# Where the second branch's gate sums meet the tokens' factor: at the PSUM eviction, or after their return from DRAM

## Chip, cores and metric

The kernel runs on one core of one Trainium2 chip. The metric is the device time of one execution in microseconds, taken as the median of the runs; lower is better.

## What is computed

The reference is one layer of a decoder trunk: 512 tokens, 1024 channels, fp32. Cut to what matters here:

```python
h = rms_norm(x, norm_mix)
proj = h @ w_in                      # split into rq, rk, rv, rg, cq, ckv, krope, gr, gm
a_ret = (rms_norm(retention(rq, rk, rv)) * silu(rg)) @ w_br
a_mla = attention(cq, ckv, krope) @ w_bm
mixed = sigmoid(gr) * a_ret + sigmoid(gm) * a_mla
x = x + mixed @ w_o                  # then an MLP, then a gated input embedding
```

`rms_norm` multiplies each token's row by one number, the reciprocal root of its mean square, and each channel by a gain. The kernel uses that a token's factor can be taken out of a product: it multiplies `w_in` by x with the gains only, and applies the factor to the result. In the kernel the tensors lie turned, channels on the 128 partitions and the 512 tokens along the free axis, so the tokens' factor is a full 128x512 tile, `rbc`, whose rows are all alike. The change concerns `gm`, the gate of the attention branch: 1024 channels, that is eight tiles of 128x512.

## The kernel before

Every matrix product is made of three TensorE products: each operand is split into a high and a low part (`split` for activations, lines 302 to 314; `load_chunk` for weights, lines 247 to 269), and `mm3` (line 292) multiplies low by high, high by low and high by high, recorded as line 169. For each chunk of weights ScalarE writes the high part (`wh_...`, line 262) and VectorE the low part (`wl_...`, line 266). So TensorE waits for ScalarE and then VectorE ahead of each chunk, unless they are early. Three weight chunks can be in their split form at a time (`NW`), six in the raw form.

The work is a list of steps in one order (`step`, `fill`, lines 1181 to 1414). First come the latent projections, then the attention heads, two at a time. Between the parts of the attention the list puts "fillers" (line 1181): the half products of the gates `gm` and `gr`, which depend on nothing but x and their weights, so that TensorE has work while VectorE and ScalarE do the softmax. `gate_m` (line 679) adds up one gate tile in a PSUM bank in two such halves. After the second half `gate_out` (line 686) empties the bank into an SBUF tile `zm`, and `aside` (line 352) writes that to DRAM with a DMA issued by GpSimd. Tile 0 is the exception: its products come before the factor `rbc` exists, so its `gate_out` is a step of its own, after `x_factor` (line 460), which makes `rbc` with a ScalarE copy.

When all heads are done, `branch_m` (line 694) runs eight times: it loads one gate tile back from DRAM over SyncE's queue into a tile `gb`, takes the sigmoid on ScalarE, multiplies it by the branch's product `bm` in PSUM on VectorE and puts the result aside again (`am`). Between these steps `norm_x` (line 708) normalises x with `rbc` for the retention part that follows. `rbc` is also used by `gate_r` (line 903) for the other gate.

Three things set the order. TensorE's matmuls, the sines and the sigmoid of `branch_m` are wrapped in `keep_in_program_order` and stay in the order of the list. All other instructions are placed by the tile framework's planner when the program is built: each engine gets one fixed queue, in which an instruction that the planner thought ready may stand ahead of one that is written earlier. And an SBUF tile of the pool `dyn` (45 tiles of 128x512, handed out by `T`) or a PSUM bank (8, handed out by `B`) is free again only when its last reader is done, a DMA among them.

Other names that the prediction uses: `v00h`, `v00l` and the like are the split attention values (line 542); `o`, `qt`, `sa`, `sb` belong to the rotation of the queries (`rotary_out`, lines 550 to 570), which runs once for each group of four heads; `tra` and `trs`, `trc` are the angles and their sine and cosine for the retention part (`trig`, lines 466 to 480, and `sincos`, line 486); `hr` and `nsc` are a pair of heads' factors (`pair_stats`, line 591), `kf` is a head's factor for the keys (line 613); `sc` the scores, `p` and `mx` the scaled scores and their maximum (line 644), `pt` the turned probabilities; `sqk` a square of the keys (line 527).

Of the kernel before, what the change touches and what calls it, by code (L numbers as in the profile page):

```python
# [33 lines left out]
AF = mybir.ActivationFunctionType  # L34
ALU = mybir.AluOpType
# [113 lines left out]
def trunk_layer(ctx: ExitStack, tc: tile.TileContext, xT, pT, pos, gains, const, decay, wstream, outT):  # L149
# [15 lines left out]
    TT, STT, TS = nc.vector.tensor_tensor, nc.vector.scalar_tensor_tensor, nc.vector.tensor_scalar  # L165
    ACT = nc.scalar.activation
# [4 lines left out]
    def T(name, dtype=F32):  # L171
        return dyn.tile([P, S], dtype, tag="t", name=name)
# [4 lines left out]
    def B(name):  # L177
        return psum.tile([P, S], F32, tag="ps", name=name)
# [113 lines left out]
    def mm3(ps, stat, mov, first, last, **k):  # L292

        (sh, sl), (mh, ml) = stat, mov
        MM(ps, sl, mh, start=first, stop=False, **k)
        MM(ps, sh, ml, start=False, stop=False, **k)
        MM(ps, sh, mh, start=False, stop=last, **k)

    def cut(pair, a, n=P):
        return pair[0][:, a:a + n], pair[1][:, a:a + n]  # L300
# [15 lines left out]
    def proj(ps, acts, w, base=0, stride=P, k0=0, k1=None):  # L316

        n = len(acts)
        for k in range(k0, n if k1 is None else k1):
            mm3(ps, cut(w, base + (k - k0) * stride), acts[k], k == 0, k == n - 1)  # L320
        return ps
# [28 lines left out]
    V = {}  # L350

    def aside(name, t):

        d = spill.tile([P, S], F32, tag=name, name=name + "d")
        nc.gpsimd.dma_start(d, t)
        return d
# [320 lines left out]
    gate_ps = {}  # L677

    def gate_m(w, n, half):
        if half == 0:  # L680
            gate_ps[n] = B(f"gm{n}")
        proj(gate_ps[n], xg, w, k0=4 * half, k1=4 * half + 4)
        if half == 1 and n:
            gate_out(n)

    def gate_out(n):
        t = T(f"zm{n}")
        TT(t, gate_ps[n], V["rbc"], op=ALU.mult)
        zm[n] = aside(f"zm{n}", t)

    def mo_split(h):
# [2 lines left out]
    def branch_m(w, n):  # L694
        t = T(f"gb{n}")
        nc.sync.dma_start(t, zm[n])
        ps = proj(B(f"bm{n}"), mo, w)
        tc.keep_in_program_order(ACT(t, t, AF.Sigmoid))
        TT(t, t, ps, op=ALU.mult)
        zm[n] = aside(f"am{n}", t)  # L700
# [503 lines left out]
    step(("v", 0), value_pair, 0)  # L1204
    step(None, x_factor)
    step(None, gate_out, 0)
    step(("qr", 0), query_rotary, 0)
    step(None, mask_parts)
# [66 lines left out]
    for n in range(8):  # L1275
        step(("bm", n), branch_m, n)
        if n < 6:
            step(None, norm_x, 2 + n)
        if n == 3:
            step(None, x_operand, 7)  # L1280
# [177 lines left out]
```

## Time and profile before

| what | value |
|---|---|
| median of 3 runs | 1101.72 us (1101.19 to 1101.97) |
| the profiled execution, its own time | 1101.0 us |
| its span, first to last instruction | 1099.2 us |
| mean granted TensorE clock | 0.999 |
| VectorE busy | 757.9 us, 69% of the span |
| ScalarE busy | 565.8 us, 51% |
| GpSimd busy | 111.1 us, 10% |

The profile is one execution, with every instruction's start and duration in microseconds from the span's start. Engines are PE (TensorE; PEld is its weight load), DVE (VectorE), ACT (ScalarE), POOL (GpSimd) and SP (SyncE, which issues DMAs; SPq is its queue). A row names the line of the kernel, the operation, out<-in, and shapes. In rows of the timeline the first number is the start, the second the duration, and a bracket at the end gives how long the engine had been idle and what ended the wait. Rows of groups have a count (x8), the busy time and the mean duration in ns. Matmuls are pipelined, so that a duration is longer than the step from one to the next.

### The profile page before, as it was taken

Reading aid. Unit: us, or ns where it says so; the run is one execution under the profiler, and the core shown is the slowest. Engines: PE = TensorE matmul, PEld = TensorE weight load, DVE = VectorE, ACT = ScalarE, POOL = GpSimd, SP = SyncE. Lnnn points to the kernel's source line nnn. Section 1 sums busy time; section 2 is a strip of 40 time slices with the busy share of each in tenths; the row PEclk is TensorE's granted clock in tenths of the full one; section 3 lists DMA queues with packets and bytes.
Section 4 is the critical chain, followed back from the end, with each engine's and each line's share of the span. In section 5 each row is a group of like instructions: output and inputs, shape, how many; then the busy total and the mean of one; then the engine's idle time right before and its main releaser. Section 6 shows DMA issues by size and latency. Waiting matters only on the chain. (4 is left out here: it accounts for less than half of the span.)

```text
span 1099.2 us, 14887 instructions
## 1 busy us (share of the span) xinstructions
PE 1085.2 (99%) x5569; PEld 923.3 (84%) x5569; DVE 757.9 (69%) x1176; ACT 565.8 (51%) x817; POOL 111.1 (10%) x145
## 2 busy tenths in 40 slices
PE   9999999999999999999999999999999999999998
PEld 7778888888888888888888888887899899898887
DVE  7697677566774655655465467649869769769784
ACT  7647656444466545344554644426645545546541
POOL 0000000000112001122100100011111111201000
PEclk9999999999999999999999999999999999999999
DMA  7232231356778744498864934694998999979511
GB/s 261 71 120 87 72 107 50 133 199 212 206 190 241 193 157 159 121 196 213 204 205 118 286 126 148 199 305 117 229 267 222 229 272 220 238 217 279 154 47 58
DMA packets 64616, 195.91 MB, mean 178 GB/s; under 512 B 7904, under 2 KB 9312, under 8 KB 64160
## 3 DMA queue, kind: packets, MB, share of 16 engines
q1 hardware_dynamic: 46464, 134.90, 35.7%
q0 software_dynamic: 17936, 60.04, 27.3%
q8 instruction: 44, 0.72, 0.3%
q14 instruction: 28, 0.23, 0.1%
q10 hardware_dynamic: 144, 0.03, 0.0%
HBM read 175.80 MB, written 17.04 MB: 175 GB/s over the span
## 5 line engine op out<-in xcount | busy, mean ns | idle before, releaser
L169 PE MATMUL dn<-wl_dn,ch 128*128 128x512 f32 x224 | 87.7, 391 | 1.5 <-DVE wl_dn L266 1.5
L169 PE MATMUL dn<-wh_dn,cl 128*128 128x512 f32 x224 | 87.7, 391 | 1.4 <-DVE cl L308 0.9
L169 PE MATMUL dn<-wh_dn,ch 128*128 128x512 f32 x224 | 87.2, 389 | 0.0
L262 ACT ACTIVATE wh_up<-wr_up 128x1024 fp32r<-128x1024 f32 x32 | 33.9, 1058 | 44.1 <-PE us L169 13.4
L266 DVE TENSOR_TENSOR wl_up<-wr_up,wh_up 128x1024 fp32r<-128x1024 f32 x32 | 39.1, 1221 | 24.4 <-ACT wh_up L262 24.0
L262 ACT ACTIVATE wh_dn<-wr_dn 128x1024 fp32r<-128x1024 f32 x32 | 33.9, 1059 | 34.1 <-PE us L169 16.5
L169 PEld LDWEIGHTS dn<-wh_dn,cl 128*128 128x128 f32 x224 | 42.1, 188 | 10.5 <-DVE cl L308 1.3
L169 PEld LDWEIGHTS dn<-wl_dn,ch 128*128 128x128 f32 x224 | 42.1, 188 | 10.3 <-DVE wl_dn L266 2.3
L169 PEld LDWEIGHTS dn<-wh_dn,ch 128*128 128x128 f32 x224 | 42.1, 188 | 8.8
L266 DVE TENSOR_TENSOR wl_dn<-wr_dn,wh_dn 128x1024 fp32r<-128x1024 f32 x32 | 39.0, 1220 | 10.7 <-ACT wh_dn L262 10.6
L262 ACT ACTIVATE wh_rv<-wr_rv 128x1024 fp32r<-128x1024 f32 x28 | 29.7, 1059 | 30.6 <-issue 9.9
L262 ACT ACTIVATE wh_rg<-wr_rg 128x1024 fp32r<-128x1024 f32 x28 | 29.6, 1059 | 30.4 <-PE rg L169 12.1
L266 DVE TENSOR_TENSOR wl_rg<-wr_rg,wh_rg 128x1024 fp32r<-128x1024 f32 x20 | 24.5, 1226 | 23.5 <-ACT wh_rg L262 23.4
L224 POOL DMA_DIRECT2D dr_dn<-wstream x24 | 21.9, 957 | 173.2 <-DVE rx L331 95.9
L266 DVE TENSOR_TENSOR wl_dn<-dr_dn,wh_dn 128x1024 fp32r<-128x1024 f32 x24 | 29.3, 1220 | 13.9 <-ACT wh_dn L262 13.9
L266 DVE TENSOR_TENSOR wl_rv<-wr_rv,wh_rv 128x1024 fp32r<-128x1024 f32 x20 | 24.4, 1223 | 16.2 <-ACT wh_rv L262 16.2
L266 DVE TENSOR_TENSOR wl_br<-wr_br,wh_br 128x1024 fp32r<-128x1024 f32 x16 | 19.5, 1221 | 19.7 <-ACT wh_br L262 19.7
L1105 DVE TENSOR_TENSOR d<-d,dn 128x1024 f32<-128x1024 f32 x24 | 29.2, 1217 | 5.4 <-PE dn L169 5.4
L262 ACT ACTIVATE wh_up<-dr_up 128x1024 fp32r<-128x1024 f32 x18 | 19.1, 1062 | 25.9 <-PE dn L169 14.1
L262 ACT ACTIVATE wh_dn<-dr_dn 128x1024 fp32r<-128x1024 f32 x24 | 25.3, 1053 | 13.1 <-PE dn L169 6.5
L262 ACT ACTIVATE wh_br<-wr_br 128x1024 fp32r<-128x1024 f32 x16 | 16.9, 1058 | 21.0 <-issue 12.8
L873 ACT ACTIVATE rt<-br 128x512 f32<-128x512 f32 x24 | 13.9, 594 | 25.8 <-PE br L169 25.8
(1889 smaller groups left out, 3690.2 us busy)
## 6 DMA issues: line engine op xcount, KB each, us to landing
wr_up<-wstream SPq DMA_DIRECT2D x32, 512.0 KB, 5.6
wr_dn<-wstream SPq DMA_DIRECT2D x32, 512.0 KB, 6.9
dr_dn<-wstream POOLq DMA_DIRECT2D x24, 512.0 KB, 9.5
wr_rv<-wstream SPq DMA_DIRECT2D x20, 512.0 KB, 4.1
wr_rg<-wstream SPq DMA_DIRECT2D x20, 512.0 KB, 5.0
dr_up<-wstream POOLq DMA_DIRECT2D x18, 512.0 KB, 9.0
wr_rv<-wstream POOLq DMA_DIRECT2D x16, 512.0 KB, 6.5
wr_rg<-wstream POOLq DMA_DIRECT2D x16, 512.0 KB, 6.9
```

Of the source, the lines that this page charges most:

```text
L169: return tc.keep_in_program_order(nc.tensor.matmul(*a, **k))
L224: nc.gpsimd.dma_start(raw, chunk(("w", blk, kb, fb, c)), accum_op=ALU.add)
L262: i = ACT(hi, raw, AF.Copy, scale=sign)
L266: TT(lo, raw, hi.bitcast(F32), op=ALU.subtract)
L873: ACT(t, ps, AF.Copy)
L1105: TT(to, to, dps[p], op=ALU.add if sign > 0 else ALU.subtract)
```

## The change

`gate_out` no longer multiplies by `rbc` on VectorE as it empties the bank; ScalarE copies the sums as they are, and they go to DRAM so. `branch_m` multiplies the tile by `rbc` on VectorE after it is back in SBUF, ahead of the sigmoid. Nothing else is edited; the step that empties tile 0 stays after `x_factor`, though its copy no longer reads `rbc`.

```diff
     def gate_out(n):
         t = T(f"zm{n}")
-        TT(t, gate_ps[n], V["rbc"], op=ALU.mult)
+        ACT(t, gate_ps[n], AF.Copy)
         zm[n] = aside(f"zm{n}", t)
...
     def branch_m(w, n):
         t = T(f"gb{n}")
         nc.sync.dma_start(t, zm[n])
+        TT(t, t, V["rbc"], op=ALU.mult)
         ps = proj(B(f"bm{n}"), mo, w)
         tc.keep_in_program_order(ACT(t, t, AF.Sigmoid))
         TT(t, t, ps, op=ALU.mult)
```

## The prediction

> **What bounds the kernel now.** I read the page first: engine shares and the granted clock.
>
> ```profile
> PE 1085.2 (99%) x5569; PEld 923.3 (84%) x5569; DVE 757.9 (69%) x1176; ACT 565.8 (51%) x817; POOL 111.1 (10%) x145
> ...
> PEclk9999999999999999999999999999999999999999
> ```
>
> TensorE is busy 99% at full clock; no instruction of its is touched. The change can gain only TensorE's idle time, 14.0 us of the span of 1099.2. Next I asked for TensorE's waits in the stretch where the gate tiles are made (40 to 149 us), and for busy time by stage: us of the stage, then PE, PEld, DVE, ACT.
>
> ```profile
> PE gm L169 <- DVE wl_gm L266: 1.6, 1, 1.6
> PE sc L169 <- ACT sqk L527: 0.8, 1, 0.8
> PE pt0a L169 <- DVE p L653: 0.6, 1, 0.6
> PE gm L169 <- DVE mx L644: 0.6, 1, 0.6
> ```
>
> ```profile
> 90.00:103.00 13.00, 11.55 (x63) 9.69 (x62) 10.65 (x30) 12.31 (x26) 0.00 (x0) 1.00 0.21 62
> ...
> 285.00:738.00 453.00, 453.00 (x2067) 377.87 (x2066) 271.05 (x396) 221.63 (x324) 52.15 (x66) 1.00 0.68 190
> 738.00:775.00 37.00, 34.34 (x167) 28.02 (x166) 36.01 (x42) 24.43 (x30) 3.48 (x4) 1.00 0.59 153
> ```
>
> Four waits, 3.6 us together, lie where VectorE loses the eight multiplications. From 285 to 738 us TensorE is never idle, and where the multiplications come back (232 to 283 us) its waits list nothing either: what is saved or lost ahead shifts the rest unchanged, and added VectorE work costs nothing unless it outlasts its cover.
>
> **What moves, and its price.** The instruction that leaves and those that resemble what comes:
>
> ```profile
> L688 DVE TENSOR_TENSOR zm<-gm,rbc x8: 681/692/692, 61.7 to 176.4; 128x512 f32<-128x512 f32 x8
> ```
>
> ```profile
> 61.09 0.60 ACT L463 ACTIVATE rbc<-prx 128x512 f32<-128x512 f32 x1
> 61.57 0.49 ACT L310 ACTIVATE v00h<-pv,f 128x256 fp32r<-128x256 f32 x1
> ...
> 62.28 0.62 ACT L553 ACTIVATE sa<-pqa 128x512 f32<-128x512 f32 x1
> ```
>
> ```profile
> 61.27 0.48 DVE L313 SCALAR_TENSOR_TENSOR v01l<-pv,f,v01h 128x256 fp32r<-128x256 f32 x1
> 61.72 0.69 DVE L688 TENSOR_TENSOR zm<-gm,rbc 128x512 f32<-128x512 f32 x1
> 62.33 0.48 DVE L313 SCALAR_TENSOR_TENSOR v00l<-pv,f,v00h 128x256 fp32r<-128x256 f32 x1
> ...
> 63.11 0.74 DVE L556 SCALAR_TENSOR_TENSOR o<-pqa,gn,tmc 128x512 f32<-128x512 f32 x1
> ...
> 65.74 0.68 DVE L560 TENSOR_TENSOR o<-o,qt 128x512 f32<-128x512 f32 x1
> ...
> 68.15 0.68 DVE L266 TENSOR_TENSOR wl_gm<-wr_gm,wh_gm 128x512 fp32r<-128x512 f32 x1
> ```
>
> ```profile
> 68.98 0.47 PE L169 MATMUL gm<-xg0h,wl_gm 128*128 128x512 f32 x1 [1.56 <-DVE wl_gm L266]
> ```
>
> A multiplication holds VectorE 0.61 us (61.72 to the next start at 62.33); eight free 4.9 us ahead of 177 us. Eight return in branch_m, at 0.6 to 0.7 each by the SBUF row of 65.74. ScalarE gains eight copies out of PSUM: `rbc` is such a copy, and the next instruction starts 0.48 us after it, so 3.8 us. Engine totals do not set the end; the four waits do.
>
> *First wait (68.98).* VectorE works without a break from 61.27, and the weights' low part is last in that queue, at 68.15. With zm0 gone it could come 0.61 sooner, but v00l then waits for ScalarE's v00h (61.57 + 0.49 = 62.06 against its start at 62.33), and `o` for `sa`, which reads the same product and ends at 62.90 against 63.11. I take 0.2, between 0 and 0.6. The copy itself needs no `rbc`, and tile 0's last product starts at 45.19, so the planner can place it 15 us earlier; if it stays among these rows it takes the 0.2 back.
>
> ```profile
> 45.19 0.39 PE L169 MATMUL gm<-xg7h,wh_gm 128*128 128x512 f32 x1
> ...
> 112.26 0.39 PE L169 MATMUL gm<-xg7h,wh_gm 128*128 128x512 f32 x1
> ```
>
> *Second and third waits.* One chain ends both.
>
> ```profile
> 82.21 0.17 DVE L605 TENSOR_SCALAR nsc<-hr 128x8 f32<-128x8 f32 x1
> 82.68 0.69 DVE L688 TENSOR_TENSOR zm<-gm,rbc 128x512 f32<-128x512 f32 x1 [0.30 <-PE gm L169]
> 83.29 0.48 DVE L468 TENSOR_SCALAR tra<-posf,cst 128x512 f32<-128x512 f32 x1
> ...
> 88.10 0.43 DVE L479 TENSOR_SCALAR tra<-tra 128x512 f32<-128x512 f32 x1
> ```
>
> ```profile
> 88.57 0.63 ACT L487 ACTIVATE trs<-tra 128x512 f32<-128x512 f32 x1 [5.21 <-DVE tra L479]
> ...
> 89.62 0.58 ACT L613 ACTIVATE kf<-pbk 128x512 f32<-128x512 f32 x1
> ...
> 100.28 0.61 ACT L527 ACTIVATE sqk<-pk 128x512 f32<-128x512 f32 x1
> ```
>
> ```profile
> 97.39 0.66 PE L169 MATMUL pt0a<-cst,p 128*128 128x128 f32 x4 [0.65 <-DVE p L653]
> ...
> 100.94 0.45 PE L169 MATMUL sc<-k1h,q1l 128*128 128x384 f32 x1 [0.81 <-ACT sqk L527]
> ```
>
> zm3 stands ahead of the angle chain (82.68), having waited 0.30 for its bank. ScalarE waits 5.21 us for that chain and then works almost without pause (12.31 of 13 us from 90 to 103), with `kf`, the softmax and `sqk` behind it; TensorE waits for these at 97.39 and 100.94. Without zm3 the angles can start when nsc is done, at 82.3 instead of 83.29: the whole chain 1.0 us earlier. TensorE can use that: ahead by 0.2 from the first wait, it has 0.65 + 0.81 = 1.46 idle here, so 1.66 is the most without a better first wait. I take 1.0 in all at 101 us (this includes the first 0.2), between 0 (a tile slot for `tra` comes free no sooner) and 2.0. No gate copy falls among ScalarE's 90 to 103 us: zm3's is due at 82.5, inside the 5.21 idle, and zm4's last product starts only at 112.26 (the second row above).
>
> *Fourth wait.* Here the copy may hurt.
>
> ```profile
> 137.82 0.69 DVE L688 TENSOR_TENSOR zm<-gm,rbc 128x512 f32<-128x512 f32 x1 [0.30 <-PE gm L169]
> ...
> 141.40 0.75 DVE L556 SCALAR_TENSOR_TENSOR o<-pqa,gn,tmc 128x512 f32<-128x512 f32 x1 [2.23 <-DMA zm5d<-zm]
> ```
>
> ```profile
> 137.82 0.64 ACT L262 ACTIVATE wh_gm<-wr_gm 128x512 fp32r<-128x512 f32 x1 [1.20 <-PE gm L169]
> ...
> 140.97 0.59 ACT L554 ACTIVATE sb<-pqb 128x512 f32<-128x512 f32 x1
> ```
>
> ```profile
> 138.80 0.54 POOL L355 DMA_DIRECT2D zm5d<-zm  x1 [24.59 <-DVE zm L688]
> ```
>
> ```profile
> 148.09 0.47 PE L169 MATMUL gm<-xg0h,wl_gm 128*128 128x512 f32 x1 [0.65 <-DVE mx L644]
> ```
>
> `o` takes over zm5's tile and waits 2.23 us until the DMA has emptied it; nine VectorE steps later the maximum `mx` is what TensorE waits for. On ScalarE the copy becomes ready at the same moment as wh_gm, which is written earlier and goes first: 0.54 later, less 0.09 because a copy is 0.60 and not 0.69 long, gives 0.45 more wait. Between a gain of 0.65 (`o` gets another tile) and a loss of 3.75 (the copy goes behind `sb`, ending at 141.56: a rival below). I take a loss of 0.45.
>
> *branch_m.* The added multiplication stands between the load and the sigmoid, and VectorE's queue waits with it for the landing.
>
> ```profile
> 259.69 1.22 DVE L266 TENSOR_TENSOR wl_bm<-wr_bm,wh_bm 128x1024 fp32r<-128x1024 f32 x1 [2.34 <-ACT wh_bm L262]
> ```
>
> ```profile
> L169 PE MATMUL bm<-mos0h,wl_bm x8: 389/389/396, 231.1 to 269.2; 128*128 128x512 f32 x8
> ```
>
> ```profile
> DMA to landing us min/median/max: 2.7/4.2/5.9
> ```
>
> The last branch's weights, split at 260.9, are first used at 269.2, and the reload landed within 5.9 (rows of bm and of gb): 8.3 us of cover, against 0.6 plus at most the slowest landing, 5.9, which sum to 6.5. Cost nothing; were the cover gone, a tile would cost 0.6. Behind the multiplication queue x's splits and the next low parts, ahead of the same cover. `rbc` keeps its tile some 6 us longer (last read by the last branch_m, not norm_x); no wait for a tile is listed there, so nothing, at most one such load.
>
> The Trainium skill, "VectorE: DVE Perf Modes", Rules for kernel authors, speaks against the edit: work on a matmul's output should be done from PSUM directly, or after a copy only if many operations follow. One follows here, so by it the sum would be 0 saved on VectorE and 3.8 us more on ScalarE. "Perfetto Trace Analysis", Optimizing Scalar/DVE Operations, speaks for it: move work to ScalarE where VectorE is saturated. The trace bears out the second from 61.27 to 68.83 and neither elsewhere, since TensorE covers it.
>
> *Sum.* Profiled execution 1101.0 (span 1099.2 and 1.8 around it), less 1.0, plus 0.45: 1100.45. The runs' median lies 0.72 above that execution: 1101.2.
>
> **Rivals.** *All four waits go:* with VectorE lighter the planner puts the angles or `kf` sooner, and `o` takes another tile. For it: TensorE's scores are ready long before `kf`. Against: three separate bits of luck. 3.6 us less: 1098.1.
>
> *Slower, the late copy of zm5:* the planner puts it behind `sb`, at 141.56 instead of 137.82. `o`, which needs its tile, follows 3.75 us later, and TensorE at 148.09 too: 1101.0 - 1.0 + 3.75 + 0.72 = 1104.5. It decides once the copy is over 3.2 us late. For it: `o` already waits. Against: from the end of wh_gm at 138.46 to `sb` at 140.97 ScalarE has only one other instruction, `sa`.
>
> *Given back:* `tra` still waits for its tile, the first wait stays, zm5 costs 0.45: 0 to 0.5 more, 1101.7 to 1102.2.
>
> *Another order far on:* from 738 to 775 us VectorE is full (36.01 of 37) and TensorE idle 2.66. If the planner's list differs there, that may vanish, on top of the sum 1098.5, or double, on top of no gain 1101.0 + 2.66 + 0.72 = 1104.4.
>
> *A table load for each copy* would cost far more, but the trace has `rbc`, a copy, between two sines with no load listed, so nothing is left for it.
>
> **Numbers.** The forecast has 0.50, given back 0.15, all waits gone 0.14, late copy 0.10, another order 0.11 (half each way). This kernel's measurement tells about 0.2% from no change, 2.2 us: faster is below 1099.5, slower above 1103.9. Faster 0.14 + 0.05 = 0.19, slower 0.10 + 0.06 = 0.16, within 0.65. The range runs from 1098.5 to 1104.0; it leaves out the late copy, the other order's slower half and the far end of the first rival.
>
> **What would show it.** Right: in TensorE's waits the one of 1.6 shrinks a little, those of 0.6 and 0.8 by about 0.8 together, `trs` starts near 87.6; `o` still waits for zm5's DMA, a little longer; no wait from 149 to 738 us; zm0 is copied before 60 us. Wrong: a new wait in 230 to 285 us, ScalarE copies ahead of `kf` or `sqk` that delay them, `o` no longer waiting for a DMA, or the 738 to 775 stretch with other idle time than 2.66.

## The result, and the profile after

| | before | changed |
|---|---|---|
| median of 11 runs each, on one chip | 1101.55 us (1100.96 to 1102.85) | 1104.31 us (1103.12 to 1107.3) |
| ratio, 95% interval | | 1.0027 (1.0018 to 1.0036) |
| the profiled execution's span | 1099.2 us | 1103.8 us |

The changed kernel is slower by 2.8 us. The forecast was 1101.2, within a range of 1098.5 to 1104.0; it was wrong, by a loss that it had priced at nothing.

The page of the changed kernel, busy times and granted clock:

```profile
PE 1087.5 (99%) x5569; PEld 924.3 (84%) x5569; DVE 758.5 (69%) x1176; ACT 570.7 (52%) x825; POOL 110.8 (10%) x145
...
PEclk9999999999999999999999999999999999999999
```

Nothing shows here: VectorE has as much to do as before (eight multiplications out, eight in), ScalarE 4.9 us more. TensorE's waits from 40 to 149 us, where the multiplications left:

```profile
PE gm L169 <- DVE wl_gm L266: 1.9, 1, 1.9
PE sc L169 <- ACT sqk L527: 0.8, 1, 0.8
PE gm L169 <- DVE mx L644: 0.4, 1, 0.4
PE pt0a L169 <- DVE p L653: 0.2, 1, 0.2
```

In order of time, the second of the four (`pt0a`) and the fourth (`mx`) shrank, and the first grew. And from 149 to 738 us, where there was no wait at all before:

```profile
PE rq L169 <- ACT xn7h L307: 2.4, 1, 2.4
...
PE rq L169 <- DVE xn7l L308: 0.2, 1, 0.2
```

`rq` is the first product of the retention part; its operand is the normalized x, eight tiles, and it waits for the last of them. The timeline of VectorE, then ScalarE, then TensorE there, each row with the start, the duration and in brackets the idle time and what ended it:

```profile
279.95 0.69 DVE L697 TENSOR_TENSOR gb<-gb,rbc 128x512 f32<-128x512 f32 x1 [2.08 <-DMA gb<-zm5d]
281.13 0.75 DVE L713 SCALAR_TENSOR_TENSOR xr<-xr,gn,rbc 128x512 f32<-128x512 f32 x1 [0.48 <-DMA xr<-xT]
...
282.57 0.69 DVE L308 TENSOR_TENSOR xn7l<-xr,xn7h 128x512 fp32r<-128x512 f32 x1
```

```profile
280.68 0.63 ACT L699 ACTIVATE gb<-gb 128x512 f32<-128x512 f32 x1 [4.07 <-DVE gb L697]
281.91 0.63 ACT L307 ACTIVATE xn7h<-xr 128x512 fp32r<-128x512 f32 x1 [0.60 <-DVE xr L713]
```

```profile
282.60 0.50 PE L169 MATMUL rq<-xn7h,wl_rq 128*128 128x512 f32 x1 [2.37 <-ACT xn7h L307]
283.32 0.50 PE L169 MATMUL rq<-xn7l,wh_rq 128*128 128x512 f32 x1 [0.22 <-DVE xn7l L308]
```

Two things could be meant by these rows. VectorE stands 2.08 us at the new multiplication until gate tile 5 has landed, and ScalarE 4.07 us behind it at the sigmoid: the added instruction holds both queues. But right after it x's own last tile, xr7, is waited for too (0.48): it also came late. SyncE's queue says why. The kernel before, then the changed one:

```profile
266.82 0.37 SPq L696 DMA_DIRECT2D gb<-zm5d  x1
267.29 0.38 SPq L711 DMA_DIRECT2D xr<-xT  x1
```

```profile
272.89 0.41 SPq L696 DMA_DIRECT2D gb<-zm5d  x1
273.41 0.55 SPq L712 DMA_DIRECT2D xr<-xT  x1
```

Loads go out in a rhythm of one weight chunk in some 5.4 us, a gate tile and an x tile behind most of them. In the changed kernel's queue the pair stands one chunk further back. And there it also takes longer. Issues with KB and us to landing, from the stretch after the pair's issue, of the kernel before and of the changed one:

```profile
gb<-zm5d SPq DMA_DIRECT2D x1, 256.0 KB, 3.7
xr<-xT SPq DMA_DIRECT2D x1, 256.0 KB, 4.2
```

```profile
wr_rv<-wstream POOLq DMA_DIRECT2D x1, 512.0 KB, 6.6
gb<-zm5d SPq DMA_DIRECT2D x1, 256.0 KB, 7.0
xr<-xT SPq DMA_DIRECT2D x1, 256.0 KB, 7.7
am4d<-gb POOLq DMA_DIRECT2D x1, 256.0 KB, 6.2
```

Issued 6.1 us later and landed 3.5 us slower, xr7 is there at 281.1 instead of 271.5. In the changed kernel the DMA engines' share (the last column but one) reaches 1.00 while it is on its way:

```profile
274.00:278.00 4.00, 4.00 (x19) 3.33 (x18) 3.72 (x7) 1.42 (x2) 0.56 (x1) 1.00 0.96 265
278.00:282.00 4.00, 2.23 (x10) 1.50 (x8) 1.56 (x3) 0.72 (x2) 0.88 (x1) 1.00 1.00 383
```

The kernel before has as full a stretch there (1.02 from 274 to 278 us), but its xr7 had landed at 271.5, ahead of it.

The Trainium skill, "DMA: Bandwidth & Descriptors", Issuing engines are not separate DMA queues, says that DMAs of SyncE, ScalarE and GpSimd end on the same 16 engines and interleave; the rows agree, as GpSimd's two transfers here are slow as well (6.6 and 6.2; their like behind the earlier load took 5.3 and 3.9).

A measure that all kernels share is the stretch from the first matmul of `rq` (xn0h) to the first of `rk` (xn0h): 274.66 to 285.54 before, 10.88 us; 275.30 to 289.39 after, 14.09 us. That is 3.21 more: the 2.6 of waits, and a slow restart (the two matmuls above lie 0.72 apart, 0.22 of it idle, where the undisturbed step is 0.23).

The rest of the changed kernel's profiled time is in two other places. At 68.97 the longer first wait is followed by a lower clock, the column after POOL's:

```profile
68.00:72.00 4.00, 3.03 (x10) 2.45 (x11) 3.94 (x7) 0.60 (x2) 0.56 (x1) 0.79 0.55 163
72.00:76.00 4.00, 4.00 (x22) 2.76 (x22) 1.70 (x6) 0.71 (x2) 0.00 (x0) 0.78 0.41 102
```

The first experiment has the same wait without a lower clock, so the wait does not bring it in every execution; whether it brings it more often is taken up at the end. And between 742 and 764 us 0.6 us are lost, whose cause the same experiment shows.

### The profile page after: what moved, and what is told of

Read it like the earlier page. It is cut to its first block, busy times and chain, and to the rows that moved or that the text cites. A ratio compares the mean times of both kernels' runs of the same rounds, so it can differ in the third digit from the quotient of the medians.

```text
span 1103.8 us, 14884 instructions
## 1 busy us (share of the span) xinstructions
PE 1087.5 (99%) x5569; PEld 924.3 (84%) x5569; DVE 758.5 (69%) x1176; ACT 570.7 (52%) x825; POOL 110.8 (10%) x145
```

## The experiments

Two theories stood. **L**: the loads of x's tiles go out a weight chunk later, and that alone makes xr7 late. **M**: the multiplication holds VectorE and the sigmoid until the gate tile has landed, and xn7 queues behind. The first expectations call the two together A, the multiplication in `branch_m` as the cause. Rivals to both: the copies on ScalarE (**B**), and VectorE's added work as such (**W**). Twelve kernels ran on three chips, four at a time beside the kernel before (medians there 1102.11, 1101.56 and 1101.82 us), with eleven runs each, and five or six for four of them (multiplication behind the sigmoid, first copy early, x early first attempt, both early).

**One half of the change alone: the copies.** From the changed kernel:

```diff
         nc.sync.dma_start(t, zm[n])
-        TT(t, t, V["rbc"], op=ALU.mult)
         ps = proj(B(f"bm{n}"), mo, w)
```

> The copies on ScalarE as in the changed kernel, the multiplication in branch_m left out (so the factor is missing ahead of the sigmoid). Theory A, the 2.6 us idle ahead of rq come from the multiplication in branch_m alone: no wait at rq, first wait (at 68 us) still 1.9 instead of 1.6, angle chain still earlier: 1101 to 1102 where the granted clock keeps at 0.999, and some 1.7 us more in the runs in which it falls behind the longer first wait, as it did in about half of the runs of the changed kernel; median 1101.0 to 1103. Rival B, the copies on ScalarE shift the whole order of the loads: the 2.6 at rq stay, 1103.5 to 1104.5.

Measured: 1102.06 us, ratio 1.0001 (0.9992 to 1.0010), no wait from 149 to 738 us, the stretch 10.88. B falls. This kernel has no lowered clock at 68 us, so what the copies do is clean here. First wait, angle chain (VectorE, ScalarE), and the waits behind it:

```profile
68.98 0.47 PE L169 MATMUL gm<-xg0h,wl_gm 128*128 128x512 f32 x1 [1.89 <-DVE wl_gm L266]
96.91 0.66 PE L169 MATMUL pt0a<-cst,p 128*128 128x128 f32 x4 [0.21 <-DVE p L653]
100.45 0.44 PE L169 MATMUL sc<-k1h,q1l 128*128 128x384 f32 x1 [0.81 <-ACT sqk L527]
...
147.38 0.47 PE L169 MATMUL gm<-xg0h,wl_gm 128*128 128x512 f32 x1 [0.43 <-DVE mx L644]
```

```profile
81.47 0.83 DVE L266 TENSOR_TENSOR wl_kq<-wr_kq,wh_kq 128x640 fp32r<-128x640 f32 x1 [0.28 <-issue]
82.21 0.48 DVE L468 TENSOR_SCALAR tra<-posf,cst 128x512 f32<-128x512 f32 x1
...
140.61 0.75 DVE L556 SCALAR_TENSOR_TENSOR o<-pqa,gn,tmc 128x512 f32<-128x512 f32 x1 [1.44 <-ACT sa L553]
```

```profile
61.96 0.63 ACT L688 ACTIVATE zm<-gm 128x512 f32<-128x512 f32 x1
62.43 0.64 ACT L553 ACTIVATE sa<-pqa 128x512 f32<-128x512 f32 x1
...
87.50 0.63 ACT L487 ACTIVATE trs<-tra 128x512 f32<-128x512 f32 x1 [3.74 <-DVE tra L479]
...
137.32 0.60 ACT L688 ACTIVATE zm<-gm 128x512 f32<-128x512 f32 x1 [1.19 <-PE gm L169]
137.82 0.62 ACT L262 ACTIVATE wh_gm<-wr_gm 128x512 fp32r<-128x512 f32 x1
```

Against the kernel before, TensorE is 0.49 us ahead at the third wait (100.94), 0.71 at the fourth (148.09), and 0.96 at the first matmul of `rq` (274.66 to 273.70); it stays 0.97 ahead until 742 us. Then it loses most of it again, by 764 us. VectorE in the kernel before and in this one, then TensorE in both:

```profile
738.99 0.75 DVE L994 SCALAR_TENSOR_TENSOR x2n<-x2n,gn,bcx 128x512 f32<-128x512 f32 x1 [2.32 <-DMA x2n<-x2d]
```

```profile
738.87 0.75 DVE L994 SCALAR_TENSOR_TENSOR x2n<-x2n,gn,bcx 128x512 f32<-128x512 f32 x1 [2.28 <-DMA x2n<-x2d]
```

```profile
763.88 0.50 PE L169 MATMUL dn<-wl_dn,ch 128*128 128x512 f32 x1 [1.50 <-DVE wl_dn L266]
```

```profile
763.76 0.50 PE L169 MATMUL dn<-wl_dn,ch 128*128 128x512 f32 x1 [1.51 <-DVE wl_dn L266]
```

The same matmul starts 0.12 earlier, not 0.97. VectorE's rows say why. `x2n`, an operand of the MLP, is loaded back from DRAM; VectorE stands idle until it has landed, and then works without a pause up to the low part that this matmul waits for. The two loads of x2n were issued 0.96 us earlier (719.39 against 720.35), but took 16.5 us to land (median) against 15.7, so VectorE's row, too, starts only 0.12 earlier. In the profiles of all fourteen kernels this row and this matmul are shifted against the kernel before by the same amount, to 0.02 us: the changed kernel by 4.49 and 4.50, the control below by 1.06 and 1.07. So this stage starts when the load lands, and what TensorE gained ahead is lost there unless the load lands sooner as well. Why the landing moves from kernel to kernel, the runs don't show.

The two rows of TensorE also show that the clock isn't decided by the length of a wait alone: after 1.50 and 1.51 us of the same wait, the next 4 us had the full clock in the kernel before and 0.57 here.

```profile
764.00:768.00 4.00, 4.00 (x17) 3.10 (x18) 4.00 (x5) 4.00 (x5) 2.62 (x3) 1.00 0.43 71
```

```profile
764.00:768.00 4.00, 4.00 (x12) 3.09 (x12) 4.00 (x5) 4.00 (x5) 2.61 (x3) 0.57 0.51 60
```

**The other half alone: the multiplication.** From the changed kernel:

```diff
-        ACT(t, gate_ps[n], AF.Copy)
+        TT(t, gate_ps[n], V["rbc"], op=ALU.mult)
         zm[n] = aside(f"zm{n}", t)
```

> The gate sums multiplied on VectorE as before, and the changed kernel's multiplication in branch_m as well (so the factor is applied twice). Theory A: wait at rq 2.4 + 0.2 as in the changed kernel, first wait 1.6 as before, granted clock 0.999 in every run: 1104.0 to 1104.5. Rival B: no wait at rq, 1101.5.

Measured: 1103.93 us, ratio 1.0017 (1.0008 to 1.0026). xr7 goes out at 273.39 and takes 6.1 us; the wait at `rq` is 0.7 + 0.2 in the profiled execution, the stretch 12.41. So this half carries the loss, some 1.9 of 3.0 us by the ratios; the wait is smaller than expected because the load landed 1.6 us sooner than in the changed kernel.

**The multiplication behind the sigmoid.** From the last kernel:

```diff
-        TT(t, t, V["rbc"], op=ALU.mult)
         ps = proj(B(f"bm{n}"), mo, w)
         tc.keep_in_program_order(ACT(t, t, AF.Sigmoid))
         TT(t, t, ps, op=ALU.mult)
+        TT(t, t, V["rbc"], op=ALU.mult)
```

> As the run with the multiplication alone, but it stands behind the sigmoid, on the product with the branch's matmul (so the factor is applied twice, the second time in the wrong place): VectorE has the same eight extra multiplications in the same stretch, and rbc is held as long, but nothing stands between the load and the sigmoid. Theory A1, what costs is that VectorE and the sigmoid wait for the load's landing and the loads are put behind a weight chunk: no wait at rq over 0.3, 1101.5. Rival A2, the extra 5 us of VectorE's work and the longer hold of rbc's tile are the cost: wait at rq 0.6 to 2.6, 1102 to 1104.

Measured: 1105.07 us, ratio 1.0031 (1.0019 to 1.0042), wait 1.1 + 0.4, stretch 12.96. A1 falls as it was put. But the run does not prove A2 either: here too xr7 went out late, at 272.83, with no multiplication ahead of the sigmoid. Any extra VectorE step in the branch, it seems, moves the loads; so the loads had to be moved by themselves.

**Loads late, no multiplication.** From the kernel before:

```diff
     for n in range(8):
         step(("bm", n), branch_m, n)
-        if n < 6:
-            step(None, norm_x, 2 + n)
-        if n == 3:
+        if 0 < n < 7:
+            step(None, norm_x, 1 + n)
+        if n == 4:
             step(None, x_operand, 7)
```

> The kernel before, without any multiplication in branch_m, but with each norm_x from the fourth tile on one branch later, so that the load of xr7 is issued one weight chunk (some 5.5 us) later, near 273, as in the changed kernel, while the loads of the gate tiles keep their places. Theory L, what TensorE waits for at rq is the late load of xr7 and nothing else: wait at rq 0.7 to 2.6 without a single multiplication, 1102.3 to 1104.5. Rival M, it is the multiplication that holds VectorE and the sigmoid until gb5 has landed: no wait at rq over 0.3, 1101.5 to 1102.

Measured: 1104.03 us, ratio 1.0027 (1.0018 to 1.0035), the changed kernel's own ratio, without one of its edits. The loads of this kernel, and its waits from 149 to 738 us:

```profile
266.29 0.37 SPq L696 DMA_DIRECT2D gb<-zm5d  x1
...
272.51 0.49 SPq L711 DMA_DIRECT2D xr<-xT  x1
```

```profile
PE rq L169 <- ACT xn7h L307: 1.9, 1, 1.9
PE rq L169 <- DVE xn7l L308: 0.2, 1, 0.2
```

This is what L forecast, and M isn't needed for the loss. The edit delays the normalization of x together with its load; the runs below with the loads in steps of their own move the load alone.

**Gate tile early, x late.** In the changed kernel the load of `gb` becomes a step of its own, one branch ahead:

```diff
...
+    step(None, gate_in, 0)
     for n in range(8):
+        if n < 7:
+            step(None, gate_in, n + 1)
         step(("bm", n), branch_m, n)
```

> The changed kernel with the load of each gate tile one branch earlier, so that the multiplication finds gb5 landed (issued near 267), while xr7 is still loaded near 273. Theory L: wait at rq still 0.7 to 2.6, near the changed kernel, 1103 to 1104.3. Rival M: the wait at rq goes, below 0.3, and the time falls to 1101.2 to 1102.

Measured: 1103.95 us, ratio 1.0018 (1.0009 to 1.0027), wait 1.3 + 0.4. With gb5 landed long before, VectorE waits for x itself:

```profile
278.80 0.75 DVE L716 SCALAR_TENSOR_TENSOR xr<-xr,gn,rbc 128x512 f32<-128x512 f32 x1 [2.21 <-DMA xr<-xT]
279.47 0.68 DVE L700 TENSOR_TENSOR gb<-gb,rbc 128x512 f32<-128x512 f32 x1
```

M falls: the multiplication now stands behind the late tile, and the wait is still there.

**x early, first attempt.** In the changed kernel:

```diff
+    step(None, norm_x, 2)
     for n in range(8):
         step(("bm", n), branch_m, n)
-        if n < 6:
-            step(None, norm_x, 2 + n)
+        if n < 5:
+            step(None, norm_x, 3 + n)
```

> The changed kernel with norm_x one branch earlier: xr7 is loaded near 267 as in the kernel before and normalized ahead of gb5's multiplication, while gb5 is still loaded near 273 and the eight multiplications stand where they did. Theory L: no wait at rq over 0.3, 1101 to 1102. Theory M as well, as far as gb5's multiplication no longer stands ahead of xr7. Rival W, VectorE's added work of 5 us is the cost: wait at rq 0.5 to 2.6, 1102 to 1104.

Measured: 1106.67 us, ratio 1.0043 (1.0030 to 1.0055). The edit did not do what it was made for: xr7 went out at 272.50, and the wait was 1.0 + 0.2. It also made waits of 2.4 us in all for `rv`'s weights, which no other kernel has. As a test of the theories it says only that late loads go with the wait.

**x early, second attempt.** In the changed kernel the loads of x and of the gate tiles become steps of their own; `branch_m` and `norm_x` take the loaded tile, and keep the multiplication:

```diff
...
+    for k in range(2):
+        step(None, load_x, k)
     step(None, norm_x, 0)
     step(None, norm_x, 1)
     step(None, mo_split, MH - 1)
+    for n in range(2):
+        step(None, gate_in, n)
     for n in range(8):
         step(("bm", n), branch_m, n)
+        if n + 2 < 8:
+            step(None, gate_in, n + 2)
+        if n + 2 < 8:
+            step(None, load_x, n + 2)
         if n < 6:
             step(None, norm_x, 2 + n)
```

> The changed kernel with nothing but the loads of branch_m and norm_x in steps of their own, x two and the gate tiles two branches ahead: all eight multiplications stay, xr7 is put behind the same weight chunk as in the kernel before (issued near 267), gb5 earlier than there. Theory L, the late load of xr7 is the whole cost: no wait at rq over 0.3, first wait still 1.9, 1100.5 to 1102.3, within 0.2% of the kernel before. Rival M or W, the multiplication or VectorE's added work costs by itself: wait at rq 0.5 or more, 1102.5 to 1104.

Measured: 1101.82 us, ratio 1.0003 (0.9994 to 1.0012). No wait from 149 to 738 us, the stretch 10.88. x's load, and VectorE there:

```profile
266.95 0.33 SPq L716 DMA_DIRECT2D xr<-xT  x1
```

```profile
270.00 0.69 DVE L700 TENSOR_TENSOR gb<-gb,rbc 128x512 f32<-128x512 f32 x1 [0.47 <-DMA gb<-zm7d]
...
271.75 0.74 DVE L721 SCALAR_TENSOR_TENSOR xr<-xr,gn,rbc 128x512 f32<-128x512 f32 x1
```

All eight multiplications are there, VectorE even waits 0.47 for a landing, and the loss is gone. L holds; M and W fall.

> As the last run, with the gate tiles loaded one branch ahead instead of two; xr7 then goes out one weight chunk ahead of its place in the kernel before (near 262). Theory L: as the last run, no wait at rq, 1100.5 to 1102.3; the place of gb's load makes no difference. Rival M: 1102.5 to 1104.

The same, with the gate tiles one branch ahead:

```diff
-    for n in range(2):
+    for n in range(1):
         step(None, gate_in, n)
...
-        if n + 2 < 8:
-            step(None, gate_in, n + 2)
+        if n + 1 < 8:
+            step(None, gate_in, n + 1)
```

Measured: 1101.86 us, ratio 1.0004 (0.9995 to 1.0013), xr7 at 262.57, stretch 10.88. Where the gate tile's load stands makes no difference. This kernel and that of "Gate tile early, x late" both load the gate tiles one branch ahead and keep all eight multiplications; they differ in the place of x's loads alone, and their ratios are 1.0004 and 1.0018.

> The kernel before with the same early loads, without the change: the control for the three above. If the early loads are worth nothing where no load is late: 1101.5, within 0.1% of the kernel before, and the run with the loads back minus this one is what the change itself is worth, between -1 and +0.5 us. If they help or hurt elsewhere, this one shows by how much.

The control, the same edit as in the run that brought the loads back, in the kernel before, whose `branch_m` has no multiplication. Measured: 1102.24 us, ratio 1.0002 (0.9993 to 1.0010), stretch 10.88. So the early loads are worth nothing that can be measured where none was late, and neither is the change without its late loads.

**Tile 0's copy.** Three kernels moved it. Early, as soon as its product is done:

```diff
-        if half == 1 and n:
+        if half == 1:
             gate_out(n)
...
     step(None, x_factor)
-    step(None, gate_out, 0)
```

> The changed kernel, but tile 0 is copied as soon as its product is done, some 15 us earlier, and no longer ahead of sa. Theory C, the copy among those rows lengthens the first wait by 0.3 and the longer wait lets the granted clock fall in half of the runs: first wait 1.6 or less, granted clock 0.999 in every run, 1103 to 1103.7 with the 2.6 at rq unchanged. Rival D, the clock falls for another reason (heavier draw, or chance): the runs still split into two groups, some 1.7 us apart.

Measured: 1105.66 us, ratio 1.0041 (1.0027 to 1.0054). The first wait did shrink to 1.3, but 2.2 at `rq` stayed, and two waits appeared far on:

```profile
PE up L169 <- DVE wl_up L266: 2.3, 1, 2.3
...
PE up L169 <- DVE xr L935: 0.8, 1, 0.8
```

The longer one comes from the reload of x2n: it was issued at 723.10, took 18.9 us, and VectorE stood idle 5.95 us for it (2.93 in the kernel before). The runs do not split into two groups (clock 0.998 in four of five, 0.996 in one), but the 0.999 that C forecast came in none of the five, and in the profiled one the clock fell behind the wait of 2.3: neither C nor D is shown. Late, behind `sa` and `sb`, with the loads as in the run that brought them back:

```diff
-    step(None, gate_out, 0)
...
     step(None, rotary_out, 0)
+    step(None, gate_out, 0)
```

> The loads as two runs above, and tile 0's copy put behind sa and sb. If the copy ahead of sa is what made the first wait longer: first wait 1.6 or less, no wait at rq, 0.3 us less than two runs above, 1100.2 to 1102; if the rows of VectorE decide: 1.9 unchanged.

Measured: 1101.54 us, ratio 1.0002 (0.9993 to 1.0011). The wait for the weights became one of 1.4 for the copy itself, since TensorE needs the bank, and 0.3 appeared behind it: 1.7 for 1.9.

> The last run's edit together with tile 0's early copy: the version that should be best by theory L. First wait 1.3, no wait at rq, 1100.5 to 1101.5, if the new wait of 2.3 + 0.8 us at up (740 to 750 us), which the early copy alone had, came from the planner's order and not from the early copy; 1103 to 1104 if it stays.

The early copy's edit together with that of the failed first attempt. Measured: 1108.98 us, ratio 1.0061 (1.0049 to 1.0074), the slowest of all. xr7 went out at 272.34 again, a wait of 2.7 with a clock of 0.50 to 0.67 behind it, and `up` waited 2.5.

All kernels side by side, from their SyncE, DMA and TensorE rows; the issue of xr7 is counted from the first matmul of `rq`:

| kernel | multiplication in branch_m | xr7 issued, us | us to landing | stretch rq to rk, us | ratio to before |
|---|---|---|---|---|---|
| before | no | -7.4 | 4.2 | 10.88 | 1 |
| changed | yes | -1.9 | 7.7 | 14.09 | 1.0027 |
| copies alone | no | -7.4 | 4.1 | 10.88 | 1.0001 |
| multiplication alone | yes | -1.9 | 6.1 | 12.41 | 1.0017 |
| behind the sigmoid | after it | -1.9 | 6.5 | 12.96 | 1.0031 |
| first copy early | yes | -1.9 | 7.4 | 13.70 | 1.0041 |
| loads late | no | -1.6 | 6.6 | 13.63 | 1.0027 |
| gate load early | yes | -1.9 | 6.6 | 13.15 | 1.0018 |
| x early, failed | yes | -1.6 | 6.0 | 12.64 | 1.0043 |
| both early | yes | -1.8 | 7.9 | 17.09 | 1.0061 |
| loads back | yes | -7.1 | 4.1 | 10.88 | 1.0003 |
| loads ahead | yes | -11.4 | 4.2 | 10.88 | 1.0004 |
| loads back, copy late | yes | -7.1 | 3.9 | 10.88 | 1.0002 |
| before, loads ahead | no | -11.7 | 4.2 | 10.88 | 1.0002 |

The stretch follows the third column and not the second. Among the late ones it also follows the landing. Third and fourth column together give the time at which xr7 is there, counted from the first matmul of `rq`; its own first product is due 4.76 us after that matmul, and the tile must be normalized and split before. It is there at 4.2 us in the multiplication alone, then 4.4, 4.6, 4.7, 5.0, 5.5, 5.8 and 6.1 (both early), and the stretch grows in the same order, 12.41, 12.64, 12.96, 13.15, 13.63, 13.70, 14.09 and 17.09. What the runs don't settle is how an added VectorE step leads the planner to put the loads behind one more weight chunk. No version beats the kernel before.

## Why the prediction was wrong

**The step that failed** is "Cost nothing" for `branch_m`. Its cover, 8.3 us, was computed for the branch's own weights, `wl_bm`, and those were indeed early. The late operand was another one, x's last tile, which `norm_x` loads over the same queue of SyncE. "Behind the multiplication queue x's splits" was written, but x's own load was not followed: that it went out at 267.29, 7.4 us ahead of `rq`, and that its place in SyncE's queue depended on what the planner made of the branch. The price of that is 3.2 us in the profiled execution. The list of what would prove the prediction wrong named it first, a new wait in 230 to 285 us; none of the rivals did. "Another order" was looked for at 738 us, where VectorE is full, and came in SyncE's queue.

**The eviction's side was about right in its sum**, -0.55 at the fourth wait against -0.71 measured, but from terms that were each off, so that the nearness of the sum is in part luck. The first wait: the copy stayed among those rows and, as the prediction said for that case, took the gain back; `wl_gm` starts at 68.15 as before, TensorE arrives 0.32 earlier and waits that much longer. The angles: `trs` came at 87.50, forecast near 87.6, but half of the 1.0 reached TensorE (0.49), because the wait for `sqk` kept its 0.81. The place that zm3 left in VectorE's queue was taken by a split, `wl_kq`, at 81.47, which had stood ahead of `nsc` before. The fourth wait: 0.45 more was forecast, 0.22 less came. The copy of zm5 went ahead of `wh_gm`, not behind it, so `o` waits for `sa` and no longer for the DMA.

**"What is saved or lost ahead shifts the rest unchanged"** held from 285 to 742 us (0.97 throughout, copies alone) and failed behind it: at 764 us 0.12 was left. The prediction quoted 36.01 of 37 us on VectorE as a stage that is full, but did not ask what that work starts on. It starts on the reload of x2n, which TensorE's coming 0.97 sooner moved by 0.12. That is the same omission as in `branch_m`: a load of the next stage that was not followed.

So the 2.8 us are 3.2 for the late load, less 0.97, plus some 0.6 behind the reload of x2n (3.85 behind at `rk`, 2.24 without 1.61 of low clock, and 0.65 more by 763.88). The 1.61 is the distance of the changed kernel's `pt0a` (98.52) from that of the copies alone (96.91).

Of the two rules that were weighed, the Trainium skill's "Perfetto Trace Analysis", Optimizing Scalar/DVE Operations (move work to ScalarE where VectorE is saturated) was right for 61 to 148 us, by 0.71. The Trainium skill's "VectorE: DVE Perf Modes", Rules for kernel authors, spoke against the edit, and the edit lost, but not for its reason: with the loads back, the extra step costs nothing that can be measured (1.0003, 0.9994 to 1.0012).

## What to carry to other kernels

When an instruction is added to a stage, ask for every operand of the next stage's first products when its load goes out and when it lands, not only for the operand that the added instruction touches; a load that is ready 7 us early is covered by its place in the queue, and the place can move. If loads and their use are one step, give the loads a step of their own. And a gain ahead of a stage that starts when a load lands is a gain at the end only as far as that load lands sooner too.

## What the runs showed of the hardware

A 256 KB load took 3.9 to 4.2 us when issued 7 us or more ahead of `rq`, and 6.0 to 7.9 when issued 1.6 to 1.9 ahead, among the next weight chunks and GpSimd's transfers: the late load was 1.8 to 4 us slower as well.

The granted clock fell behind single idle times of TensorE of 1.5 to 2.7 us, in some executions and not in others: after 1.88 at 68.97 in the changed kernel and not after 1.89 at the same matmul in the copies alone (1.00 from 68 to 76 us). In stretches of 1 us, the changed kernel's clock from 70 to 74 us was 0.67, 0.50, 0.50 and 0.62. What is missing there sums to 1.71 us, that is some 3.4 us at half clock; the 0.79, 0.78 and 0.57 shown above are means over 4 us that contain such a fall. Behind the wait of 2.74 in both early the clock stayed at 0.50 from 282 to 288 us, about twice as long.

The Trainium skill, "TensorE: Matmul & The Clock Gate", Part 1, says that the clock is decided over a window of some 3.4 us that runs on its own and isn't reset when a kernel starts. That the same wait has two outcomes, and the length of the falls, agree with that; that 1.5 us of idle time is enough goes beyond what the page says, an idle window of 3.4. What decided each case here stays open. It moves single executions by about 1.6 us, so a comparison of two profiled executions at this size needs the clock read first.

The runs suggest that the longer first wait brings such falls more often. Of the 33 executions of copies alone, loads back and loads ahead (first wait 1.9, no wait at `rq`) 11 had a mean clock of 0.997 or less; of the 22 of the two kernels with early loads and a first wait of 1.6 or 1.4 none had, and of the 76 of the kernel before beside all twelve, one. It is less clear in the changed kernel and in "Gate tile early", with the same first wait: 2 and 1 of 11. The two executions of copies alone at 0.999 took 1099.98 and 1100.50 us. So a gain of the copies may be hidden behind a lower clock. With one trace for each kernel, and two executions chosen by their clock, that is not shown.
